# Feed-forward of a two-layer block in split fp32: which of two engines makes the low parts of which weights

## The chip, the cores and the metric

The kernel runs on one core of one Trainium2 chip, in one launch. The metric is device time in microseconds (us). A core has five engines with a queue of instructions each: PE (TensorE) does the matmuls, and PEld is its weight load; DVE (VectorE), ACT (ScalarE) and POOL (GpSimd) work on tiles of 128 partitions; SP (SyncE) issues the DMA transfers. An engine runs its queue in order: an instruction that waits holds up all that stand behind it. Matmuls read SBUF and add into PSUM; DVE and ACT can read PSUM.

## What is computed

Two layers over 512 tokens and 256 context tokens of width 1024, each an attention mixer and a feed-forward, all in fp32. The feed-forward is what the change touches:

```
def swiglu(h, w_in, w_out):
    g, u = jnp.split(h @ w_in, 2, axis=-1)
    return (jax.nn.silu(g) * u) @ w_out
...
        h = h + g2 * swiglu(modulate(h, norm2_g[l], sh2, sc2), ffn_w_in[l], ffn_w_out[l])
        if need_ctx:
            hc = hc + cg2 * swiglu(modulate(hc, norm2_g[l], csh2, csc2), ffn_w_in[l], ffn_w_out[l])
```

The hidden width is 2816, which is 22 tiles of 128. The first layer computes the tokens and the context (768 columns), the second the tokens alone (512).

## The kernel before

**Split products.** Activations lie transposed: features on partitions, tokens along the free axis. To multiply at fp32 precision, each matrix is split into a high part (a cast to fp32r by ScalarE, L901) and a low part (source minus high part, L904), and `mm3` issues three matmuls: high by high (L99), high by low (L100), low by high (L101).

**Seven products for eight.** The input product of a hidden tile f is a 2 by 2 block product, done in Strassen's way with seven products (numbered 1 to 7) of half width instead of eight. `product(n, f)` issues number n. Products 1, 2 and 4 use a quarter of the raw weights as loaded (a11, a12, a22). Products 5, 6, 3 and 7 use a sum: `weights` makes it on VectorE in one tile that is overwritten each time (L926): t = a21 + a22, then t = t - a11, then t = a12 - t, then t = a11 - a21. So a sum can be made only when the split of the sum before it has been read. These tiles are called t, or sq for every third f. The tile of raw weights (1 MB, `ffn_in`, L794) has three buffers, so the load for f + 3 waits for the last reader of f.

**Emptying the accumulators.** VectorE adds the products out of PSUM into the gate and the up part (hs, and q or u): L965 after product 1, L976 after 3, L980 after 7, L982, L985 after 4. The next product into the same accumulator, or into its buffer, waits for them. Two accumulators of this kind (pw) exist, and PE interleaves the products of two tiles. Then hs is split (L115 ScalarE, L116 GpSimd).

**Output weights.** `s2` multiplies pairs of finished hidden tiles by output weights (rawo, L913; on average two splits of 128x512 a hidden tile) into three small accumulators (pb); VectorE empties each into the residual stream (L757: xT for the tokens, ctxT for the context).

**Other work on VectorE.** During the first feed-forward VectorE also computes the second layer's modulation vectors: 64 operations over 128x1024 (L220, junk).

**Who makes the low parts.** `slot` does the split. In the first layer (l = 0) all 192 low parts run on GpSimd: the raw weights of products 1 and 2 need none for f = 0, 1, 2. In the second layer (l = 1), of 198, every fourth call's low part runs on VectorE, whatever is split: 49 of them. In all 341 on GpSimd, 49 on VectorE.

**The order.** The program is written as a list of products and output blocks for each f (the strings in `ffn`), and a list scheduler with its own cost estimates sets the order of each engine's queue. The tiles 0 to 2 have a list of their own; from f = 3 on, two patterns alternate with even and odd f.

Of the kernel before, what the change touches and what calls it, by code (L numbers as in the profile page):

```python
# [6 lines left out]
F32 = mybir.dt.float32  # L7
# [4 lines left out]
ALU = mybir.AluOpType  # L12
# [14 lines left out]
class Builder:  # L27
# [814 lines left out]
    def ffn(self, l):  # L842
        tc, nc, a = self.tc, self.nc, self.a
# [51 lines left out]

        raws, sums, state = {}, {}, {}

        def slot(src, t=None):
            t = ring.tile([P, 2, 512], F32R, name=self.uid("w"), tag="w", bufs=(6, 10)[l]) if t is None else t
            with tc.issue_after(self.first_sq.ins) if self.nslot < 12 else ExitStack():  # L900
                nc.scalar.copy(t[:, 0, :], src)  # L901
            self.nslot += 1
            eng = nc.vector if l == 1 and self.nslot % 4 == 0 else nc.gpsimd
            eng.tensor_tensor(t[:, 1, :], src, t[:, 0, :].bitcast(F32), ALU.subtract)  # L904
            return t

        self.nslot = 0
# [8 lines left out]
        def weights(n, f, plain):  # L916
            if f not in raws:
                raws[f] = self.raws.pop(f) if f < 2 else self.ffn_in(l, f, ring if f % 3 == 2 else self.Rf)
                sums[f] = self.sumsq()[:, :512] if f % 3 == 2 else self.tmp("t")
            r, t = raws[f], sums[f]  # L920
            a11, a12, a21, a22 = [r[:, i * 512:(i + 1) * 512] for i in range(4)]
            for v, x, y, how in ((5, a21, a22, ALU.add), (6, t, a11, ALU.subtract), (3, a12, t, ALU.subtract),
                                 (7, a11, a21, ALU.subtract)):
                if v == n:
                    with tc.issue_after(self.last_diag.ins) if both and f < 3 and n == 5 else ExitStack():
                        nc.vector.tensor_tensor(t, x, y, how)  # L926
            if plain:
                return {1: a11, 2: a12}[n]
            return slot({1: a11, 2: a12, 4: a22}.get(n) if n in (1, 2, 4) else sums[f])

        def more(n, f, ins):

# [4 lines left out]
        def product(n, f):  # L937

            plain = n in (1, 2) and f in self.plain
            w = weights(n, f, plain)  # L940
            st = state.setdefault(f, {})
            if n == 2:
# [58 lines left out]
        def s2_weights(g, m):  # L1001

            if m % 4 == 0:
                outs[g] = load(a["ffn_out"][l, g, :, 256 * m:256 * m + 1024], 1024)
                if g == NF // 2 - 1:
                    f = NF + m // 4
                    pool = ring if f % 3 == 2 else self.Rf
                    self.big = pool.tile([P, 2048], F32R, name=self.uid("raw"), tag="raw", bufs=1 if pool is ring else 2)
            if m % 2 == 0:
                o = m % 4 * 512  # L1010
                t = self.big[:, o:o + 1024].rearrange("p (a b) -> p a b", a=2) if g == NF // 2 - 1 else None
                w2[g] = slot(outs[g][:, m % 4 * 256:m % 4 * 256 + 512], t)
            w = w2[g]
            return [(w[:, 0, c:c + P], w[:, 1, c:c + P]) for c in range(m % 2 * 256, m % 2 * 256 + 256, P)]
# [37 lines left out]
        for off, n in parts:  # L1052
            rest = []
            for m in range(KT):
# [6 lines left out]
                eng = nc.vector if both and m in (2, 3) else nc.gpsimd  # L1061
# [282 lines left out]
```

## Time and profile before

| what | us |
|---|---|
| three runs | 1690.64, 1688.33, 1688.64 (median 1688.64) |
| profiled execution: span from first to last instruction | 1687.1 |
| GpSimd low parts of L904: t 106, raw 105, rawo 74 and 7, sq 49 | 487.8 busy (341 at about 1.43 mean) |
| VectorE waiting in L926 for the weights' DMA | 31.3 (t) |
| ScalarE's casts of t waiting for VectorE's sums | 174.1 |
| first feed-forward, L904 first to last start | 424 to 942 |
| second feed-forward | about 1270 to 1650 |

The profiled execution is a run of its own: the table has its span, and of its whole time the three runs' median, 1.5 us above that span, is the nearest measure. A row of the page's waits reads "engine line <- engine line: total, times, longest": the first stood idle until the second was done. In a timeline row the bracket at the end is the engine's idle time before that instruction and what ended it. In the groups by line, the three numbers of a row are busy time, mean ns of one, and idle time before.

### The profile page before, as it was taken

The numbers are of one execution on the slowest core, as the hardware profiler recorded it, in microseconds if no ns is written. First come the engines' busy times: TensorE is split into PE (matmuls) and PEld (weight loads), VectorE is DVE, ScalarE is ACT, GpSimd is POOL, SyncE is SP. The second block draws the span as 40 slices with busy tenths as digits, with TensorE's granted clock in tenths as the row PEclk, the third lists the DMA queues.
The fourth block names the chain that finished last, engine by engine and source line by source line (L and its number), as shares of the span: only waits on it lengthen the run. The fifth ranks groups of instructions, "written<-read, shape, count | busy, mean of one in ns | idle before, by whom it ended". The sixth has DMA issues, their size and how long they took to land.

```text
span 1687.1 us, 24578 instructions
## 1 busy us (share of the span) xinstructions
PE 1559.4 (92%) x9463; PEld 1363.1 (81%) x9463; DVE 1115.4 (66%) x1994; ACT 725.7 (43%) x1464; POOL 795.6 (47%) x580
## 2 busy tenths in 40 slices
PE   6999989799899899999999998999986998999996
PEld 4776878699689889889999877767776888888886
DVE  4613778855966777667665685765669865666665
ACT  3413676433533333333333345555555444434443
POOL 0562211231575665666655427522116675656663
PEclk9999989999899999999999989999998999999998
DMA  8753100241032333443341112101140332223201
GB/s 314 292 180 136 35 1 1 88 139 62 17 134 79 134 113 113 137 147 127 126 139 49 49 51 76 50 20 38 57 157 7 119 112 77 90 98 108 88 31 50
DMA packets 47957, 161.97 MB, mean 96 GB/s; under 512 B 5472, under 2 KB 9952, under 8 KB 40160
## 3 DMA queue, kind: packets, MB, share of 16 engines
q1 hardware_dynamic: 47696, 160.28, 27.3%
q8 instruction: 74, 1.21, 0.3%
q14 instruction: 43, 0.35, 0.1%
q10 hardware_dynamic: 144, 0.13, 0.0%
HBM read 158.29 MB, written 2.10 MB: 95 GB/s over the span
## 4 chain that ended last, share of the span: by engine, by line
PE 65%; DVE 17%; DMA 5%; POOL 4%; issue 4%; ACT 3%; POOLq 0%; SPq 0%; DVEq 0%; ACTq 0%
PE pb L100 8%; PE pb L99 8%; PE pb L101 8%; PE pw L99 7%; PE pw L100 7%; PE pw L101 7%; DMA raw<-ffn_in 5%; POOL w L904 3%; PE pf L99 2%; PE pb L1199 2%; PE pf L100 2%; PE pf L101 2%; DVE t L926 2%; PE pb L1193 2%; PE pf L349 2%
## 5 line engine op out<-in xcount | busy, mean ns | idle before, releaser
L78 POOL TENSOR_TENSOR w<-raw,w 128x512 fp32r<-128x512 f32 (+1 forms) x84 | 126.6, 1515 | 233.0 <-ACT w L75 210.0
L99 PE MATMUL pw<-ax,w 128*128 128x384 f32 (+2 forms) x640 | 209.6, 332 | 17.8 <-DVE q L980 8.2
L904 POOL TENSOR_TENSOR w<-t,w 128x512 fp32r<-128x512 f32 x106 | 153.2, 1446 | 152.0 <-ACT w L901 150.5
L100 PE MATMUL pw<-ax,w 128*128 128x384 f32 (+2 forms) x640 | 209.0, 327 | 2.1 <-DVE ax L456 1.4
L101 PE MATMUL pw<-ax,w 128*128 128x384 f32 (+2 forms) x640 | 207.0, 326 | 3.1 <-DVE w L904 3.1
L757 DVE SCALAR_TENSOR_TENSOR xT<-pb,mod,xT 128x512 f32<-128x512 f32 (+3 forms) x208 | 144.0, 703 | 68.1 <-PE pb L101 67.7
L99 PE MATMUL pb<-hh,w 128*128 128x512 f32 x480 | 166.3, 361 | 14.3 <-ACT hh L115 7.9
L99 PE MATMUL pw<-T,w 128*128 128x384 f32 (+1 forms) x504 | 159.4, 320 | 18.0 <-DVE hs L976 9.8
L904 POOL TENSOR_TENSOR w<-raw,w 128x512 fp32r<-128x512 f32 x105 | 148.7, 1425 | 56.0 <-ACT w L901 55.8
L100 PE MATMUL pb<-hh,w 128*128 128x512 f32 x480 | 172.8, 362 | 0.7 <-POOL hh L116 0.2
L101 PE MATMUL pb<-hh,w 128*128 128x512 f32 x480 | 168.8, 359 | 0.0
L100 PE MATMUL pw<-T,w 128*128 128x384 f32 (+1 forms) x504 | 160.1, 318 | 5.8 <-POOL T L116 3.7
L901 ACT CAST w<-t 128x512 fp32r<-128x512 f32 x120 | 74.3, 621 | 207.7 <-DVE t L926 174.1
L101 PE MATMUL pw<-T,w 128*128 128x384 f32 (+1 forms) x504 | 159.2, 316 | 0.0
L99 PEld LDWEIGHTS pw<-ax,w 128*128 128x128 f32 x640 | 123.6, 194 | 32.4 <-DVE q L980 12.0
L100 PEld LDWEIGHTS pw<-ax,w 128*128 128x128 f32 x640 | 124.3, 194 | 9.5 <-DVE ax L456 3.1
L101 PEld LDWEIGHTS pw<-ax,w 128*128 128x128 f32 x640 | 124.1, 194 | 6.8 <-DVE w L904 3.3
L904 POOL TENSOR_TENSOR w<-rawo,w 128x512 fp32r<-128x512 f32 x74 | 106.9, 1445 | 40.0 <-ACT w L901 40.0
L99 PEld LDWEIGHTS pw<-T,w 128*128 128x128 f32 x504 | 97.6, 195 | 25.4 <-DVE hs L976 11.8
L99 PEld LDWEIGHTS pb<-hh,w 128*128 128x128 f32 x480 | 89.9, 190 | 27.5 <-ACT hh L115 9.0
L99 PE MATMUL pb<-ax,w 128*128 128x256 f32 (+1 forms) x340 | 104.7, 310 | 3.9 <-ACT w L75 1.6
L100 PEld LDWEIGHTS pw<-T,w 128*128 128x128 f32 x504 | 98.5, 195 | 10.6 <-POOL T L116 5.1
(387 smaller groups left out, 4216.0 us busy)
## 6 DMA issues: line engine op xcount, KB each, us to landing
raw<-ffn_in SPq DMA_DIRECT2D x44, 1024.0 KB, 5.0
ar<-ada SPq DMA_DIRECT2D x24, 1024.0 KB, 7.2
ar<-ada SPq DMA_DIRECT2D x48, 512.0 KB, 3.5
rawo<-ffn_out SPq DMA_DIRECT2D x44, 512.0 KB, 3.8
raw<-odd_out SPq DMA_DIRECT2D x32, 256.0 KB, 2.7
raw<-qk SPq DMA_DIRECT2D x16, 256.0 KB, 7.8
raw<-uv SPq DMA_DIRECT2D x16, 256.0 KB, 2.8
raw<-even_out SPq DMA_DIRECT2D x8, 512.0 KB, 3.5
```

Of the source, the lines that this page charges most:

```text
L78: eng.tensor_tensor(lo, raw, hi.bitcast(F32), ALU.subtract)
L99: mm(out, s[0], m[0], start=start, stop=False, **kw)
L100: mm(out, s[0], m[1], start=False, stop=False, **kw)
L101: mm(out, s[1], m[0], start=False, stop=stop, **kw)
L349: nc.tensor.matmul(ps[32 * q:32 * q + 32, :w], cst[:, k, :], t[:, w * q:w * q + w], start=k == 0, stop=k == KT - 1, skip_group_check=True)
L757: self.nc.vector.scalar_tensor_tensor(h, ps[:, r], self.modcol(l, j, m, who), h, ALU.mult, ALU.add)
L901: nc.scalar.copy(t[:, 0, :], src)
L904: eng.tensor_tensor(t[:, 1, :], src, t[:, 0, :].bitcast(F32), ALU.subtract)
L926: nc.vector.tensor_tensor(t, x, y, how)
L1193: nc.tensor.transpose(pt[:, x * P:(x + 1) * P], es[2 * (x % 2) + x // 2][:, kb * P:(kb + 1) * P], self.ident)
L1199: nc.tensor.matmul(po[64 * h:64 * h + 64, :], V[vb][:, 64 * g:64 * g + 64], t[:, h * TC:h * TC + TC], start=kb == 0, stop=kb == nb - 1, sk ...
```

## The change

`slot` takes the engine as an argument. The split of a sum (products 5, 6, 3, 7) gets VectorE where f > 2, in both layers; everything else (raw weights, output weights, and the sums of f = 0, 1, 2) goes to GpSimd. So 76 low parts of each layer, 152 in all, run on VectorE instead of 49, and 238 on GpSimd instead of 341. The lines behind 903 have a number one lower afterwards.

```
-        def slot(src, t=None):
+        def slot(src, t=None, eng=None):
             t = ring.tile([P, 2, 512], F32R, name=self.uid("w"), tag="w", bufs=(6, 10)[l]) if t is None else t
             with tc.issue_after(self.first_sq.ins) if self.nslot < 12 else ExitStack():
                 nc.scalar.copy(t[:, 0, :], src)
             self.nslot += 1
-            eng = nc.vector if l == 1 and self.nslot % 4 == 0 else nc.gpsimd
-            eng.tensor_tensor(t[:, 1, :], src, t[:, 0, :].bitcast(F32), ALU.subtract)
+            (eng or nc.gpsimd).tensor_tensor(t[:, 1, :], src, t[:, 0, :].bitcast(F32), ALU.subtract)
             return t
...
             if plain:
                 return {1: a11, 2: a12}[n]
-            return slot({1: a11, 2: a12, 4: a22}.get(n) if n in (1, 2, 4) else sums[f])
+            return slot({1: a11, 2: a12, 4: a22}[n]) if n in (1, 2, 4) else slot(t, eng=nc.vector if f > 2 else None)
```

Before, VectorE in the steady part of the first feed-forward, from the L980 of one tile (up part u_6835) over the next tile's first two sums after its start (t_6993 = t - a11, then a12 - t):

```order
L980 TENSOR_TENSOR u_6835<-u_6835,pw_6798 128x384
L220 SCALAR_TENSOR_TENSOR junk_6933,acc_64<-ar_6931,cb_3265 128x1024
L757 SCALAR_TENSOR_TENSOR ctxT_635_3303<-pb_6883,mod_67,ctxT_635_3303 128x256
L982 TENSOR_TENSOR hs_6811<-hs_6811,u_6835 128x384
L757 SCALAR_TENSOR_TENSOR xT_632_3297<-pb_6939,mod_66,xT_632_3297 128x512
L757 SCALAR_TENSOR_TENSOR ctxT_636_3305<-pb_6947,mod_67,ctxT_636_3305 128x256
L926 TENSOR_TENSOR t_6993<-t_6993,raw_6991 128x512
L985 TENSOR_TENSOR hs_6811<-hs_6811,pw_6798 128x384
L926 TENSOR_TENSOR t_6993<-raw_6991,t_6993 128x512
L757 SCALAR_TENSOR_TENSOR xT_632_3297<-pb_6955,mod_66,xT_632_3297 128x512
```

The same place after the change:

```order
L979 TENSOR_TENSOR u_6835<-u_6835,pw_6798 128x384
L220 SCALAR_TENSOR_TENSOR junk_6933,acc_64<-ar_6931,cb_3265 128x1024
L757 SCALAR_TENSOR_TENSOR ctxT_635_3303<-pb_6883,mod_67,ctxT_635_3303 128x256
L903 TENSOR_TENSOR w_7072<-t_6993,w_7072 128x512
L981 TENSOR_TENSOR hs_6811<-hs_6811,u_6835 128x384
L757 SCALAR_TENSOR_TENSOR xT_632_3297<-pb_6939,mod_66,xT_632_3297 128x512
L757 SCALAR_TENSOR_TENSOR ctxT_636_3305<-pb_6947,mod_67,ctxT_636_3305 128x256
L925 TENSOR_TENSOR t_6993<-t_6993,raw_6991 128x512
L984 TENSOR_TENSOR hs_6811<-hs_6811,pw_6798 128x384
L903 TENSOR_TENSOR w_7090<-t_6993,w_7090 128x512
L925 TENSOR_TENSOR t_6993<-raw_6991,t_6993 128x512
L757 SCALAR_TENSOR_TENSOR xT_632_3297<-pb_6955,mod_66,xT_632_3297 128x512
```

Two low parts (w_7072 of product 5, w_7090 of product 6) now stand in VectorE's queue, each ahead of the sum that overwrites what it reads.

Before, VectorE in the steady part of the second feed-forward, at the change from a pair's even tile (hs_14132) to its odd one (hs_14289, u_14309), with the first sum of a later tile (sq_14766, straight from its load):

```order
L976 TENSOR_TENSOR hs_14289<-hs_14289,pw_14276 128x256
L926 TENSOR_TENSOR t_14426<-t_14426,raw_14424 128x512
L985 TENSOR_TENSOR hs_14132<-hs_14132,pw_14119 128x256
L926 TENSOR_TENSOR sq_14766<-raw_14764 128x512
L904 TENSOR_TENSOR w_14503<-t_14426,w_14503 128x512
L980 TENSOR_TENSOR u_14309<-u_14309,pw_14276 128x256
```

After the change:

```order
L981 TENSOR_TENSOR hs_14132<-hs_14132,q_14160 128x256
L925 TENSOR_TENSOR sq_14766<-raw_14764 128x512
L903 TENSOR_TENSOR w_14485<-t_14426,w_14485 128x512
L984 TENSOR_TENSOR hs_14132<-hs_14132,pw_14119 128x256
L925 TENSOR_TENSOR t_14426<-t_14426,raw_14424 128x512
L975 TENSOR_TENSOR hs_14289<-hs_14289,pw_14276 128x256
L903 TENSOR_TENSOR w_14503<-t_14426,w_14503 128x512
L925 TENSOR_TENSOR t_14426<-raw_14424,t_14426 128x512
L903 TENSOR_TENSOR w_14531<-t_14426,w_14531 128x512
L979 TENSOR_TENSOR u_14309<-u_14309,pw_14276 128x256
```

The sum straight from the load (sq_14766) has moved ahead of L984 (the L985 of before), with a low part between them, and two more low parts stand ahead of L979 (the L980 of before).

Before, GpSimd in the opening of the second feed-forward (T tiles are split activations for product 5):

```order
L904 TENSOR_TENSOR w_12004<-t_11869,w_12004 128x512
L904 TENSOR_TENSOR w_12040<-sq_11945,w_12040 128x512
L904 TENSOR_TENSOR w_12082<-t_11869,w_12082 128x512
L904 TENSOR_TENSOR w_12099<-t_11906,w_12099 128x512
L116 TENSOR_TENSOR T_11985<-hm_11488,T_11985 128x256
L116 TENSOR_TENSOR T_11990<-hm_11487,T_11990 128x256
```

After the change:

```order
L903 TENSOR_TENSOR w_12004<-t_11869,w_12004 128x512
L903 TENSOR_TENSOR w_12022<-t_11906,w_12022 128x512
L903 TENSOR_TENSOR w_12040<-sq_11945,w_12040 128x512
L116 TENSOR_TENSOR T_11985<-hm_11488,T_11985 128x256
L116 TENSOR_TENSOR T_11990<-hm_11487,T_11990 128x256
L903 TENSOR_TENSOR w_12082<-t_11869,w_12082 128x512
```

One low part (w_12022) came over from VectorE, and the two T tiles moved ahead of w_12082 and w_12099.

More of the change, by code (lines that the diff above doesn't have):

```diff
@@ L896, in ffn, with slot @@
         raws, sums, state = {}, {}, {}
-        def slot(src, t=None):
+        def slot(src, t=None, eng=None):
             t = ring.tile([P, 2, 512], F32R, name=self.uid("w"), tag="w", bufs=(6, 10)[l]) if t is None else t
@@ L902, in slot @@
             self.nslot += 1
-            eng = nc.vector if l == 1 and self.nslot % 4 == 0 else nc.gpsimd
-            eng.tensor_tensor(t[:, 1, :], src, t[:, 0, :].bitcast(F32), ALU.subtract)
+            (eng or nc.gpsimd).tensor_tensor(t[:, 1, :], src, t[:, 0, :].bitcast(F32), ALU.subtract)
             return t
@@ L928, in weights @@
                 return {1: a11, 2: a12}[n]
-            return slot({1: a11, 2: a12, 4: a22}.get(n) if n in (1, 2, 4) else sums[f])
+            return slot({1: a11, 2: a12, 4: a22}[n]) if n in (1, 2, 4) else slot(t, eng=nc.vector if f > 2 else None)
         def more(n, f, ins):
```

## The prediction

> **What bounds the kernel now.** I read the page's totals first, then the same table cut into the two feed-forwards.
>
> ```profile
> span 1687.1 us, 24578 instructions
> PE 1559.4 (92%) x9463; PEld 1363.1 (81%) x9463; DVE 1115.4 (66%) x1994; ACT 725.7 (43%) x1464; POOL 795.6 (47%) x580
> 560.00:940.00 380.00, 364.89 (x2034) 340.31 (x2033) 259.94 (x384) 127.76 (x232) 234.38 (x155) 0.99 0.34 116
> 1270.00:1380.00 110.00, 92.99 (x592) 83.80 (x592) 94.57 (x133) 53.67 (x116) 74.55 (x55) 0.92 0.22 77
> 1380.00:1640.00 260.00, 244.52 (x1640) 223.83 (x1639) 157.23 (x228) 112.63 (x229) 161.51 (x120) 0.98 0.25 86
> ...
> L976 DVE TENSOR_TENSOR hs<-hs,pw 128x384 f32<-128x384 f32 x16 | 8.9, 554 | 43.4 <-PE pw L101 43.4
> L976 DVE TENSOR_TENSOR hs<-hs,pw 128x256 f32<-128x256 f32 x16 | 6.6, 412 | 2.6 <-PE pw L101 2.6
> ```
>
> The rows with a colon give a stretch, its length, and the busy time of PE, weight load, DVE, ACT and POOL. In the first feed-forward's steady part (560 to 940) PE stands still for 380.00 - 364.89 = 15.1 us; in the second's (1380 to 1640) for 15.5 us; in the second's opening (1270 to 1380) for 17.0 us. L976 runs once a hidden tile, so each steady part holds 16 tiles, or 8 of the pairs in which the products are interleaved. The change adds no matmul and drops none, so it can only win from these gaps, or widen them. The first feed-forward's opening uses the hidden tiles 0 to 2, whose splits stay on GpSimd. PE's waits in the two steady parts:
>
> ```profile
> PE pb L99 <- ACT hh L115: 6.8, 2, 3.5
> PE pb L99 <- DVE xT L757: 4.3, 5, 1.2
> PE pw L99 <- DVE q L980: 2.4, 2, 1.2
> ...
> PE pw L99 <- DVE q L980: 5.1, 4, 2.4
> PE pw L99 <- DVE hs L985: 3.9, 4, 1.2
> PE pw L99 <- DVE hs L976: 3.2, 1, 3.2
> PE pw L99 <- DVE u L980: 2.5, 2, 2.4
> ```
>
> The first three rows are of 560 to 940, the other four of 1380 to 1640 (us in total, times, longest). Nearly all of them name a VectorE instruction that empties an accumulator. So VectorE's lateness, not a late weight, is what costs PE time; not one row names a low part. The question is whether the change makes VectorE earlier or later at those few instructions.
>
> **What a low part costs on each engine.**
>
> ```profile
> L904 POOL TENSOR_TENSOR w<-t,w x106: 1257/1298/2292, 424.1 to 1645.9; 128x512 fp32r<-128x512 f32 x106
> L904 DVE TENSOR_TENSOR w<-raw,w x21: 677/1305/1786, 1275.6 to 1631.6; 128x512 fp32r<-128x512 f32 x21
> L904 DVE TENSOR_TENSOR w<-t,w x14: 673/688/1747, 1280.6 to 1642.8; 128x512 fp32r<-128x512 f32 x14
> DVE t L926: 35.2, 31
> DVE sq L926: 15.4, 12
> ...
> L926 DVE TENSOR_TENSOR t<-t,raw x30: 670/684/2329, 426.0 to 1633.6; 128x512 f32<-128x512 f32 x30
> L926 DVE TENSOR_TENSOR t<-raw,t x30: 673/1758/2323, 435.0 to 1641.2; 128x512 f32<-128x512 f32 x30
> ...
> L901 ACT CAST w<-t x120: 603/621/632, 423.4 to 1645.2; 128x512 fp32r<-128x512 f32 x120
> ```
>
> Durations are least/median/most in ns. Undisturbed, a low part takes 1.30 us on GpSimd and 0.69 on VectorE. The tails show contention: the same sum takes 0.68 or 1.76 us, the same low part 0.69 or 1.75, so an operation with two SBUF inputs that meets a GpSimd operation loses up to some 1.07 us, 1.65 at worst (2.33 - 0.68). The two middle rows are who waited for L904: VectorE stood still for 50.6 us because the next sum overwrites a tile whose low part GpSimd had not finished reading.
>
> **Term 1, first feed-forward, steady part.** All 4 sum splits of a tile leave GpSimd (64 in 16 tiles); VectorE gets 64 x 0.69 = 44 us more against its idle 380.00 - 259.94 = 120 us. The idle that the old order forces on it goes. One instance, VectorE's rows and then PE's:
>
> ```profile
> 687.33 1.50 DVE L926 TENSOR_TENSOR t<-raw 128x512 f32<-128x512 f32 x1 [1.90 <-POOL w L904]
> 688.76 0.54 DVE L980 TENSOR_TENSOR q<-q,pw 128x384 f32<-128x384 f32 x1
> 692.28 0.68 DVE L926 TENSOR_TENSOR sq<-sq,raw 128x512 f32<-128x512 f32 x1
> 692.88 0.54 DVE L985 TENSOR_TENSOR hs<-hs,pw 128x384 f32<-128x384 f32 x1
> 695.08 2.31 DVE L926 TENSOR_TENSOR sq<-raw,sq 128x512 f32<-128x512 f32 x1 [1.65 <-POOL w L904]
> 697.31 0.74 DVE L757 SCALAR_TENSOR_TENSOR xT<-pb,mod,xT 128x512 f32<-128x512 f32 x1
> ...
> 689.35 0.44 PE L99 MATMUL pw<-ax,w 128*128 128x384 f32 x1 [1.22 <-DVE q L980]
> 698.11 0.50 PE L99 MATMUL pb<-hh,w 128*128 128x512 f32 x1 [0.47 <-DVE xT L757]
> ```
>
> The sum waits 1.65 us for GpSimd's low part and then runs 2.31 instead of 0.68, beside GpSimd; L757 stands behind it and PE behind L757. In the new order of the same place (VectorE, first feed-forward, above) a low part stands ahead of the first sum (+0.69), and another, after L984, ahead of the second. First sum 692.97 to 693.65, ScalarE's high part to 694.3 (0.62, beside L984), low part to 695.0, second sum to 695.7, L757 at 695.7 instead of 697.31: 1.6 us early, which closes a gap of 0.47 and those of 1.1 us. Each of the three two-input operations can lose up to 1.07 us to GpSimd, and L757 is later than before when two of them do; GpSimd's busy time falls by 64 x 1.30 = 83 of 234 us, so that this is the rarer case. For the L980 gap (1.22) the 1.90 us wait goes and two lows come ahead of it (1.38), so that closes less surely. The two rows hold 4.3 + 2.4 = 6.7 us. Ends: -6.7 (all closed), and +13 (at each of 8 pairs one 1.65 us stall reaches PE). I take **-5**, near the lower end, since the two instances above both name GpSimd's low part as the idle time that made VectorE late. The 6.8 us behind ScalarE's hh I leave.
>
> **Term 2, second feed-forward, steady part.** Here every fourth split was on VectorE already: 9 splits a tile (7 of the input weights, 2 of the output weights) gave 2.25; now it makes 4. That is 1.75 x 0.69 = 1.2 us a tile more; gone is the wait for GpSimd. But these gaps come from something else:
>
> ```profile
> 1463.51 0.94 DVE L926 TENSOR_TENSOR t<-raw 128x512 f32<-128x512 f32 x1 [1.87 <-DMA raw<-ffn_in]
> 1464.38 1.75 DVE L904 TENSOR_TENSOR w<-sq,w 128x512 fp32r<-128x512 f32 x1
> 1466.05 0.41 DVE L980 TENSOR_TENSOR q<-q,pw 128x256 f32<-128x256 f32 x1
> ...
> 1496.74 0.69 DVE L926 TENSOR_TENSOR t<-raw 128x512 f32<-128x512 f32 x1 [2.88 <-DMA raw<-ffn_in]
> 1497.36 0.41 DVE L985 TENSOR_TENSOR hs<-hs,pw 128x256 f32<-128x256 f32 x1
> ...
> 1466.51 0.39 PE L99 MATMUL pw<-ax,w 128*128 128x256 f32 x1 [2.37 <-DVE q L980]
> 1497.82 0.39 PE L99 MATMUL pw<-ax,w 128*128 128x256 f32 x1 [1.23 <-DVE hs L985]
> ```
>
> A sum that waits for its weights' DMA holds up what stands behind it: in one pair of tiles a low part on VectorE and L980 (PE loses 2.37), in the next L985 alone (1.23). The new order (its lines below 903 are one lower) has one pattern in every pair: L979, L981, the sum behind the DMA, a low part, L984. So L979 is out from behind the DMA, and L984 (the old L985) gets a low part ahead of it. That part's high part is ready, and costs 0.69, or 1.75 contended. On SyncE's queue the load goes out when GpSimd's last low part of the tile three back is done; with the sums gone from GpSimd's queue and ScalarE's casts a step earlier I count it 0.5 us (one cast of 0.62) early. So each pair keeps about 1.25, plus now and then a lock wait: three gaps of 2.37 and the one of 3.2 lose 1.1 each (-4.5), eight pairs gain 0.25 (+2), together **-2.5**. Ends: -7 (the late loads no longer reach PE in the four pairs: half of the 14.7 us of the four rows), and +17 (1.07 lost twice in each of 8 pairs). New on VectorE is its wait for ScalarE: in the new order one low part in four stands right behind its own sum and waits the cast, 0.62 us. Behind it are L964, L975 and L979; two other products' matmuls cover it, unless VectorE comes late already.
>
> **Term 3, opening of the second feed-forward.** Five splits go back to GpSimd: +6.5 us there, -3.4 on VectorE.
>
> ```profile
> 1285.50 3.20 POOL L904 TENSOR_TENSOR w<-t,w 128x512 fp32r<-128x512 f32 x2 [5.61 <-ACT w L901]
> 1289.89 0.58 PE L100 MATMUL pw<-T,w 128*128 128x256 f32 x1 [2.97 <-POOL T L116]
> ```
>
> PE loses 2.97 us since two low parts (3.20) stand ahead of the T tiles; the new order puts the T tiles ahead of them. Against that, one raw low part more goes through GpSimd at 1270 to 1280, where VectorE's tiny operations of the norm wait for it. Ends -3 and +3; I take **-1**. The last group of output weights moves one low part to GpSimd: nothing, since PE works on other products there.
>
> **A rule weighed.** The rows show that contention falls on whole operations (0.69 or 1.75). The Trainium skill, page "SBUF — State Buffer", section "Who interferes with whom", states that a VectorE operation with two SBUF inputs and a GpSimd operation that reads SBUF hold a shared port exclusively, the one that starts second waiting for the first to end. The 1.07 lost agrees, against 1.30 for GpSimd's operation. By that rule the change does not make the two engines work side by side: each moved low part shortens the hold from 1.30 to 0.69, and puts the wait in the queue on which PE depends. Its outcome is the rival on the other side.
>
> **Sum.** -5 - 2.5 - 1 = -8.5: span 1687.1 to 1678.6. The runs took 1688.33 to 1690.64, median 1688.64, which is 1.5 above the profiled span: **1680**.
>
> **The rivals.**
> - *VectorE comes late (slower).* GpSimd loses 16 x 1.75 low parts of 1.30 there, 36 us, and is still busy some 125 of 260 us; a moved low part that meets it takes 1.75, and everything behind it, L984 and L979 above all, goes late. For it: the low part now stands between the late sum and L984. Price: in each of 8 pairs the 1.07 reaches PE twice, +17, less the 5 won in the first feed-forward and 1 in the opening, about +11: 1700; half of it, +5 or so: 1694. It decides once more than about half of these low parts meet GpSimd.
> - *Nothing in sum.* VectorE's waits for GpSimd turn into waits for ScalarE's cast, and what the first feed-forward wins the second loses: -2 to +2, about 1688.
> - *More than I count.* GpSimd's lighter queue also takes most of the lock waits away, the 2.37 gaps and the T wait close entirely: -6.7 - 7 - 3 = -17: 1672.
>
> **How the numbers follow.** Forecast 0.47 (1675 to 1686), VectorE late 0.23, nothing in sum 0.2, more than counted 0.1. The range of 8 in 10 runs from 1672 to 1698: it takes in the larger gain and most of the slower case. About 0.2% (3.4 us) is what a measurement of this kernel can tell from no change. Faster than 1685.3: nearly all of the forecast and the larger gain, 0.55; same: nothing in sum and the forecast's edge, 0.22; slower: 0.23.
>
> **What would show it.** Right: "DVE L926 <- POOL w L904" falls from 50.6 us to what the tiles 0 to 2 have, the gaps of PE behind L757 and L979 in 560 to 940 shrink from 6.7 us to 2 or less, PE waits for L979 in 1380 to 1640 shrink and those for L984 stay at about 1.2 each. Wrong: low parts on VectorE with a median over 1.3 us, waits of "DVE w L903 <- ACT" of tens of us, or new PE waits for pb or pw behind them.

## The result, and the profile after

| kernel | median, us | runs (least to most) | profiled span, us |
|---|---|---|---|
| before, measured with the change | 1689.64 | 4 (1688.33 to 1690.72) | 1687.1 |
| after | 1675.77 | 4 (1672.10 to 1676.44) | 1674.4 |

The ratio after to before is 0.991, interval 0.9892 to 0.9928. The profiled execution of the changed kernel is its run of 1676.23 us. The two profiled executions differ by 12.7 us, where the prediction had 8.5.

The totals at the head of the page of the changed kernel:

```profile
span 1674.4 us, 24582 instructions
PE 1550.9 (93%) x9463; PEld 1358.2 (81%) x9463; DVE 1152.9 (69%) x2097; ACT 729.3 (44%) x1464; POOL 658.4 (39%) x477
```

GpSimd lost 137 us (795.6 before) and VectorE gained 37.5 (1115.4). PE's own busy time fell by 8.5 us (1559.4) at the same 9463 matmuls, which the prediction didn't foresee. The mean granted clock of PE was 0.971 in this execution and 0.969 in that of before, so a part of it is the clock's.

The groups of L903 and L925 in the changed kernel (least/median/most in ns):

```profile
L903 POOL TENSOR_TENSOR w<-raw,w x126: 1261/1296/2246, 464.4 to 1628.7; 128x512 fp32r<-128x512 f32 x126
L903 DVE TENSOR_TENSOR w<-t,w x104: 671/693/1872, 481.3 to 1629.3; 128x512 fp32r<-128x512 f32 x104
...
DVE t L925: 3.0, 2
...
L925 DVE TENSOR_TENSOR t<-raw,t x30: 670/1078/2305, 434.1 to 1622.3; 128x512 f32<-128x512 f32 x30
```

The moved low part takes 0.69 us, as the prediction assumed. The sum a12 - t, made in the tiles called t, has a median of 1.08 us where it had 1.76. The short row is who waited for L903: of VectorE's 50.6 us behind GpSimd 3.0 are left.

PE's waits in the changed kernel, the first row of 560 to 940 us, the others of 1380 to 1640:

```profile
PE pb L99 <- ACT hh L115: 5.3, 2, 3.2
...
PE pw L99 <- DVE hs L984: 5.3, 6, 2.3
PE pw L99 <- DVE q L979: 4.2, 5, 0.9
PE pw L99 <- DVE u L979: 1.9, 2, 1.0
```

Between 560 and 940 us no wait for VectorE is left. In the second feed-forward, the four rows of 14.7 us became three of 11.4.

**Where the time came from.** The span is cut at events that each kernel has. In the feed-forwards it is cut by ScalarE's casts of hh (L115), of which each hidden tile has one (the last has two halves).

| stage | before, us | after, us | difference |
|---|---|---|---|
| to the last emptying of ctxT from pw, ahead of the first feed-forward | 400.7 | 399.8 | -0.9 |
| to the 4th hh of the first feed-forward | 117.1 | 117.5 | +0.4 |
| 4th to 10th hh | 159.2 | 154.2 | -5.0 |
| 10th to last hh | 286.3 | 276.9 | -9.4 |
| to the second mixer's first exponential (L1171) | 80.7 | 84.6 | +3.9 |
| first to last exponential | 190.0 | 190.2 | +0.2 |
| to the 4th hh of the second feed-forward | 120.3 | 123.1 | +2.8 |
| 4th to last but one hh | 304.4 | 299.6 | -4.8 |
| to the end | 28.5 | 28.5 | 0 |

The two rows of the first feed-forward that hold its gain, as windows of before (busy time of PE, weight load, VectorE, ScalarE, GpSimd, then the granted clock):

```profile
517.76:676.95 159.19, 149.13 (x825) 140.04 (x824) 120.09 (x180) 52.05 (x97) 100.00 (x62) 0.98 0.35 119
676.95:963.24 286.29, 278.99 (x1568) 259.15 (x1567) 182.04 (x271) 95.47 (x174) 168.29 (x118) 1.00 0.34 112
```

And of the changed kernel:

```profile
517.26:671.49 154.23, 147.15 (x827) 138.87 (x826) 132.97 (x206) 52.32 (x98) 59.45 (x37) 0.99 0.35 123
671.49:948.35 276.86, 276.73 (x1568) 259.84 (x1567) 191.84 (x315) 95.86 (x175) 110.56 (x73) 1.00 0.34 116
```

The second row of each has the same 1568 matmuls at the same granted clock of 1.00. PE's idle time falls from 286.29 - 278.99 = 7.3 us to 0.1: afterwards PE is busy from end to end, and nothing is left to win there by waits. Its busy time falls too, by 2.3 us; the list of PE's waits doesn't show that. The profile models where a matmul ends, so the split into busy and idle is less sure than the length of the row. In the other row idle time falls by 3.0 us and busy time by 2.0; there the granted clock went from 0.98 to 0.99, an estimate of 159.19 x 0.02 - 154.23 x 0.01 = 1.6 us, which may be most of the 2.0. But e5, e6 and e7 below take 154.4 there at 0.98, as low a clock as before has, so the row's gain isn't the clock's.

The rows of the second feed-forward, before:

```profile
1233.87:1354.15 120.28, 99.74 (x653) 88.72 (x654) 98.32 (x154) 61.32 (x137) 62.30 (x50) 0.91 0.29 103
1354.15:1658.56 304.41, 286.80 (x1913) 261.82 (x1912) 188.78 (x268) 127.41 (x262) 183.72 (x135) 0.98 0.24 82
```

After:

```profile
1223.14:1346.24 123.10, 99.94 (x671) 90.02 (x672) 100.03 (x152) 62.14 (x140) 65.54 (x52) 0.92 0.28 101
1346.24:1645.88 299.64, 283.30 (x1896) 258.47 (x1895) 197.20 (x297) 130.04 (x259) 149.68 (x106) 0.99 0.23 83
```

Here the counts warn the reader: 18 matmuls lie ahead of the border now that lay behind it (671 against 653). At 299.64 / 1896 = 0.158 us they are 2.8 us. At equal work, by this estimate, the opening stayed at 120.3 and the steady part fell to 302.5: 0 and -1.9 us. In the steady part PE's idle time fell from 304.41 - 286.80 = 17.6 us to 16.3, and the granted clock rose from 0.98 to 0.99.

### The profile page after: what moved, and what is told of

Read it like the earlier page. It is cut to its first block, busy times and chain, and to the rows that moved or that the text cites. A ratio compares the mean times of both kernels' runs of the same rounds, so it can differ in the third digit from the quotient of the medians.

```text
span 1674.4 us, 24582 instructions
## 1 busy us (share of the span) xinstructions
PE 1550.9 (93%) x9463; PEld 1358.2 (81%) x9463; DVE 1152.9 (69%) x2097; ACT 729.3 (44%) x1464; POOL 658.4 (39%) x477
## 4 chain that ended last, share of the span: by engine, by line
PE 66%; DVE 16%; DMA 6%; issue 4%; ACT 4%; POOL 4%; POOLq 0%; SPq 0%; DVEq 0%; ACTq 0%
PE pw L99 8%; PE pb L99 8%; PE pw L100 7%; PE pb L100 7%; PE pw L101 7%; PE pb L101 7%; DMA raw<-ffn_in 4%; PE pf L99 3%; PE pf L100 2%; PE pf L101 2%; PE pb L1198 2%; PE pb L1192 2%; POOL w L903 2%; DVE t L925 2%; DVE junk L220 2%
## 5 line engine op out<-in xcount | busy, mean ns | idle before, releaser
L903 POOL TENSOR_TENSOR w<-raw,w 128x512 fp32r<-128x512 f32 x126 | 173.6, 1391 | 152.2 <-ACT w L901 146.0
L903 POOL TENSOR_TENSOR w<-rawo,w 128x512 fp32r<-128x512 f32 x80 | 122.2, 1527 | 198.4 <-ACT w L901 192.2
L757 DVE SCALAR_TENSOR_TENSOR xT<-pb,mod,xT 128x512 f32<-128x512 f32 (+3 forms) x208 | 144.3, 703 | 48.2 <-PE pb L101 47.8
L99 PE MATMUL pw<-T,w 128*128 128x384 f32 (+1 forms) x504 | 159.0, 318 | 17.1 <-DVE hs L975 7.4
L100 PE MATMUL pw<-T,w 128*128 128x384 f32 (+1 forms) x504 | 159.1, 316 | 3.5 <-POOL T L116 1.8
L99 PEld LDWEIGHTS pw<-T,w 128*128 128x128 f32 x504 | 97.3, 194 | 23.6 <-ACT T L115 8.8
L116 POOL TENSOR_TENSOR hh<-hs,hh 128x768 fp32r<-128x768 f32 (+1 forms) x42 | 75.9, 1809 | 85.5 <-ACT hh L115 83.1
L903 DVE TENSOR_TENSOR w<-t,w 128x512 fp32r<-128x512 f32 x104 | 89.1, 857 | 24.4 <-ACT w L901 23.4
```

The source lines that it names most:

```text
L99: mm(out, s[0], m[0], start=start, stop=False, **kw)
L100: mm(out, s[0], m[1], start=False, stop=False, **kw)
L116: return (lo_eng or nc.vector).tensor_tensor(lo, src, hi.bitcast(F32), ALU.subtract)
L757: self.nc.vector.scalar_tensor_tensor(h, ps[:, r], self.modcol(l, j, m, who), h, ALU.mult, ALU.add)
L903: (eng or nc.gpsimd).tensor_tensor(t[:, 1, :], src, t[:, 0, :].bitcast(F32), ALU.subtract)
```

## The experiments

Each expectation was written before its run. The figures of stages are of one profiled execution each; medians and ratios of e1 to e10 come from five rounds beside the kernel before. In the table, "first" is the first feed-forward, the three rows from 400.7 to its last hh together; "to exponential" is the stretch from its last emptying of ctxT to the second mixer's first exponential (17.1 us less than in the table above); "second" is the second feed-forward's opening and steady part together.

| kernel | median, us | ratio to before (interval) | first | to exponential | second |
|---|---|---|---|---|---|
| before | | | 562.6 | 63.6 | 424.7 |
| after | 1675.77 | 0.991 (0.9892 to 0.9928) | 548.6 | 67.5 | 422.7 |
| e1: change in layer 1 alone | 1680.07 | 0.9945 (0.9928 to 0.9962) | 549.3 | 67.1 | 424.1 |
| e2: change in layer 2 alone | 1690.29 | 1.0002 (0.9989 to 1.0014) | 562.3 | 63.7 | 428.1 |
| e3: unsummed weights to VectorE | 1687.70 | 0.9995 (0.9981 to 1.0009) | 556.6 | 67.1 | 422.5 |
| e4: no overwrite, engines as before | 1688.96 | 0.9996 (0.9984 to 1.0008) | 557.6 | 66.6 | 426.5 |
| e5: change, tables loaded first | 1676.89 | 0.9926 (0.9910 to 0.9942) | 548.4 | 64.9 | 422.9 |
| e6: change, opening as before | 1673.95 | 0.9907 (0.9891 to 0.9923) | 548.8 | 67.8 | 417.7 |
| e7: e5 and e6 together | 1672.66 | 0.9904 (0.9887 to 0.9922) | 549.0 | 67.1 | 417.4 |
| e8: e3 and e4 together | 1683.38 | 0.9963 (0.9948 to 0.9978) | 553.8 | 66.8 | 422.8 |
| e9: change, no overwrite | 1687.96 | 0.9977 (0.9961 to 0.9993) | 558.9 | 64.5 | 420.9 |
| e10: e6 and e9 together | 1683.29 | 0.9955 (0.9941 to 0.9969) | 557.9 | 66.3 | 420.4 |

The second feed-forward has the same code in after, e2, e5 and e9, and their profiles spread from 420.9 to 428.1. A difference of a few us between two single profiles in that column says nothing. Before, e1, e3, e4 and e8 split there as before, and they spread from 422.5 to 426.5: the two groups have the same mean to half a us.

### One layer at a time (e1, e2)

e1, against before, beside the new argument of `slot`:

```
-            eng = nc.vector if l == 1 and self.nslot % 4 == 0 else nc.gpsimd
...
+            if eng is None and l == 1 and self.nslot % 4 == 0:
+                eng = nc.vector
...
-            return slot({1: a11, 2: a12, 4: a22}.get(n) if n in (1, 2, 4) else sums[f])
+            return slot({1: a11, 2: a12, 4: a22}[n]) if n in (1, 2, 4) else slot(t, eng=nc.vector if f > 2 and l == 0 else None)
```

e2, against the change:

```
-            return slot({1: a11, 2: a12, 4: a22}[n]) if n in (1, 2, 4) else slot(t, eng=nc.vector if f > 2 else None)
+            return slot({1: a11, 2: a12, 4: a22}[n]) if n in (1, 2, 4) else slot(t, eng=nc.vector if f > 2 and l == 1 else None)
```

> The change in the first feed-forward alone; the second splits as before (every fourth on VectorE). Theory A (the gain is won in the first feed-forward, where VectorE no longer waits for GpSimd's low part before it overwrites the sum) and rival B (it is won there by GpSimd's lighter queue) both expect about the gain that the change had at the start of the second feed-forward, -11 to -12 us, so about 1677 to 1679. Rival C (both layers share the gain evenly) expects -6 to -7, about 1683.

> The change in the second feed-forward alone; the first has all its low parts on GpSimd as before. Theory A and rival B expect -1 to -3 us (1686 to 1688), since from the opening of the second feed-forward to the end the change won only 1 to 2 us. Rival C expects -6 to -7.

e1 is 9.7 us below before (1689.76 beside it), a little less than theories A and B expected, and has the whole gain of the first feed-forward, 549.3 against 548.6. e2 can't be told from before; its -1 to -3 us did not show. So the gain is won in the first layer. What the second layer adds lies between nothing (e2 against before) and some 4 us (the change against e1).

### What in the first feed-forward was removed (e3, e4, e8)

The change does two things there: VectorE no longer waits for GpSimd before it overwrites a sum, and GpSimd has 76 low parts fewer to do. e3 takes 79 other low parts from GpSimd (of raw weights and of some output weights) and leaves the sums', so that the overwrite still waits; against before (the second layer stays as it was):

```
-            return slot({1: a11, 2: a12, 4: a22}.get(n) if n in (1, 2, 4) else sums[f])
+            return slot({1: a11, 2: a12, 4: a22}[n], eng=nc.vector if f > 2 and l == 0 else None) if n in (1, 2, 4) else slot(t)
...
+                w2[g] = slot(outs[g][:, m % 4 * 256:m % 4 * 256 + 512], t, nc.vector if l == 0 and m % 4 == 0 else None)
```

> First feed-forward: the low parts of the unsummed weights (three a tile, f > 2) and of every second output split go to VectorE, those of the sums stay on GpSimd; second feed-forward as before. 79 low parts are moved there instead of the 76 of the change, so GpSimd is relieved as much and VectorE loaded as much, but the sum is still overwritten only after GpSimd has read it. Theory A expects the waits of VectorE's sums for GpSimd to stay (over 30 us) and at most a third of the gain, -4 to +4. Rival B (lighter GpSimd queue, fewer meetings) expects about the time of the first-feed-forward-only kernel, -10 to -12.

e4 leaves the engines of before and takes the overwrite away: sums 6, 3 and 7 are written over quarters of the raw weights that nothing reads any more, and sum 7 is made a step earlier. Against before:

```
-            for v, x, y, how in ((5, a21, a22, ALU.add), (6, t, a11, ALU.subtract), (3, a12, t, ALU.subtract),
-                                 (7, a11, a21, ALU.subtract)):
+            own = l == 0 and f > 2
+            z = {5: t, 6: a11 if own else t, 3: a12 if own else t, 7: a21 if own else t}
+            for v, x, y, how in ((5, a21, a22, ALU.add), (7, a11, a21, ALU.subtract), (6, z[5], a11, ALU.subtract),
+                                 (3, a12, z[6], ALU.subtract)):
-                if v == n:
+                if v == ({6: 7, 7: 0}.get(n, n) if own else n) or own and n == 6 and v == 6:
...
-                        nc.vector.tensor_tensor(t, x, y, how)
+                        nc.vector.tensor_tensor(z[v], x, y, how)
+            t = z.get(n, t)
...
-            return slot({1: a11, 2: a12, 4: a22}.get(n) if n in (1, 2, 4) else sums[f])
+            return slot({1: a11, 2: a12, 4: a22}.get(n) if n in (1, 2, 4) else t)
```

> Engines as before in both layers. In the first feed-forward, for f > 2, the sums of products 6, 3 and 7 are written over raw quarters that are no longer needed (a11, a12, a21) instead of over the sum before, so that no sum has to wait for GpSimd's low part of the sum before; the sum of 7 is made one step earlier. Theory A expects the waits of VectorE's sums for GpSimd to fall below 20 us and -7 to -12 us. Rival B expects no gain, -2 to +2, since GpSimd's queue and the meetings are as before.

By their medians both look like nothing: e4 came out at 1688.96, as rival B expected and theory A did not. By the stages they don't. VectorE's waits for GpSimd between 560 and 940 us, before:

```profile
DVE t L926 <- POOL w L904: 17.4, 15, 2.1
DVE sq L926 <- POOL w L904: 8.0, 6, 1.7
```

In e3:

```profile
DVE t L927 <- POOL w L905: 6.6, 8, 2.1
...
DVE sq L927 <- POOL w L905: 4.4, 4, 1.7
```

In e4:

```profile
DVE sq L928 <- POOL w L904: 0.3, 1, 0.3
```

So 25.4 us before, 11.0 in e3 and 0.3 in e4 (none in the changed kernel). The windows of e4, cut as above:

```profile
521.98:683.71 161.73, 149.33 (x827) 139.95 (x826) 126.08 (x179) 52.44 (x96) 106.29 (x63) 0.98 0.35 118
683.71:959.62 275.91, 275.91 (x1568) 259.87 (x1567) 170.33 (x269) 96.48 (x174) 178.97 (x116) 1.00 0.35 116
```

In the steady row PE is busy from end to end, as in the changed kernel, while GpSimd does all its old work and is busy for 178.97 us, even more than the 168.29 of before. **That separates the two causes: in the steady part the wait before the overwrite alone cost the 9.4 us, and GpSimd's load, once that wait was gone, cost nothing.** e3 agrees from the other side. Its windows, cut at the same events:

```profile
519.45:678.57 159.12, 148.26 (x822) 137.75 (x820) 132.96 (x204) 51.40 (x95) 63.27 (x38) 0.99 0.35 120
678.57:959.24 280.67, 277.07 (x1571) 260.94 (x1572) 213.23 (x318) 96.29 (x177) 106.62 (x71) 1.00 0.34 114
```

In the second of these rows GpSimd is busy for as little as in the changed kernel (106.62 us), and VectorE still waits 4.4 + 3.7 = 8.1 us for it, where the same row of before has 13.4 + 8.0 = 21.4. Some six tenths of the wait are gone, and 5.6 us of the 9.4 are won, six tenths as well: the gain goes with the wait, and not with GpSimd's load.

What spoils e4 lies ahead of that row: 120.0 and 161.7 us where before has 117.1 and 159.2, together +5.4. Something in e4's edit costs time in the first ten tiles: the sums' new place, or sum 7 made earlier. So e4 can't say what won the change 5.0 us in the 4th to 10th tile. e3 has 159.1 there, as before, so it was not GpSimd's lighter load alone; more than that is not shown.

> First feed-forward: the low parts of the unsummed weights and of every second output split on VectorE (79 moved), and the sums written over raw quarters, so that no sum waits for GpSimd; second feed-forward as before. Apart they took 6.0 and 5.0 us off the steady part of the first feed-forward (562.6 us from the last context evacuation out of pw to the last split hidden tile). Theory G (two causes that add: the wait for GpSimd before the overwrite, and GpSimd's load with its meetings) expects about 550 to 552 us there, near the 548.6 of the change. Rival H (one cause, of which each of the two took the same part) expects 555 to 557. The time behind it keeps the 4 us at the mixer's start, so 1680 for G and 1685 for H.

e8 lies between the two expectations, because both added up whole stages. Cut as above it has 120.6, 157.9 and 275.3: the steady part is again at the floor, to which e4's edit alone had brought it, so there was nothing to add there; the first ten tiles have 278.5 against 276.3 before and 281.7 in e4.

### What is left after the change (e9, e10)

These are the change with e4's edit, and e6 with it.

> The change, and in the first feed-forward from the fourth tile on the sums of products 6, 3 and 7 are written over quarters of the raw weights that nothing reads any more, instead of over the tile of the sum before; sum 7 is made a step earlier. Theory G (the change already took away VectorE's wait before the overwrite, since low part and sum now stand in one queue; the sums' place costs nothing more): first feed-forward within 2 us of the change's 548.6 us, in all 1674 to 1678 us. Rival H (what is left of the gain hangs on how early a sum is made, since ScalarE's cast waits for it): first feed-forward 3 to 6 us shorter, 1670 to 1673 us. A third outcome: the raw weights' buffer is held longer by sums written into it, loads come later, first feed-forward 3 us or more longer.

> The kernel of e9 with, in the opening of the second feed-forward (tiles 0 to 2), every fourth low part back on VectorE as before the change. Theory G: first feed-forward within 2 us of 548.6, opening 117 to 119 us (e6 and e7 had 118.0 and 117.4; the change 123.1), in all 1672 to 1675 us, no better than e6 and e7 by more than 2 us. Rival H: 1667 to 1671 us.

Of e9's expectation only the third outcome came, and its reason is not shown. e10 missed both of its outcomes for the same loss: 1683.29 us and 557.9 in the first feed-forward. The windows of e9:

```profile
520.17:683.39 163.22, 150.83 (x825) 140.43 (x824) 132.96 (x205) 52.75 (x97) 62.37 (x37) 0.97 0.34 117
683.39:960.38 276.99, 276.08 (x1568) 259.82 (x1567) 187.72 (x313) 96.43 (x174) 105.94 (x72) 1.00 0.35 116
```

The steady row is that of the change to 0.1 us: with VectorE's wait gone, writing the sums elsewhere brings nothing there. The 4th to 10th tile take 163.2 instead of 154.2, with 5.3 us more idle time and a granted clock of 0.97 instead of 0.99 (an estimate of 163.22 x 0.03 - 154.23 x 0.01 = 3.4 us). Most of the added idle time is behind VectorE's L757, where it empties a small accumulator into xT: PE waits 5.7 us for it there, 1.2 in the change. SyncE's wait for the readers of the raw weights doesn't explain it: between 440 and 950 us it went from 45.4 us (behind GpSimd) to 50.4 (43.1 behind GpSimd and 7.3 behind VectorE). What makes VectorE late in those tiles when the sums lie in the raw weights stays open. The profiled execution of e9 took 1683.15, less than its median, so the typical loss is larger than the windows show.

### The second feed-forward's opening (e6)

Against the change:

```
+            if eng is None and l == 1 and self.early and self.nslot % 4 == 0:
+                eng = nc.vector
...
+            self.early = f < 3
```

> The change, but in the second feed-forward every fourth split of the tiles 0 to 2 has its low part on VectorE again, as before. Theory F (the opening of the second feed-forward lost about 3 us because the five splits given back to GpSimd make VectorE's small norm operations and the first products wait) expects the stretch from the last exponential to the fourth split hidden tile to fall from 123.1 to about 120.3 us, and the time by about 3 us, to 1673. Rival (noise of one profile, or the new order of the norm chain) expects 123 us and no gain.

The opening fell from 123.1 to 118.0 us, with the border back at 653 matmuls (at equal work from 120.3), and the second feed-forward in all from 422.7 to 417.7. The three kernels with this edit, e6, e7 and e10, have 417.4 to 420.4 there, less than each of the nine others (420.9 to 428.1); from e9 to e10 it is only 0.5. The trace shows one wait that the edit takes away. VectorE's timeline in the changed kernel, at the norm ahead of the second feed-forward:

```profile
1258.91 0.16 DVE L156 TENSOR_SCALAR sm<-pb 128x2 f32<-128x2 f32 x1
...
1260.53 1.25 DVE L128 TENSOR_SCALAR sm<-sm 128x2 int32<-128x2 int32 x1
1261.82 1.22 DVE L130 TENSOR_TENSOR sm<-sm 128x2 f32<-128x2 f32 x1
1263.07 1.19 DVE L131 SCALAR_TENSOR_TENSOR sm<-sm,sm 128x2 f32<-128x2 f32 x1
...
1269.17 1.19 DVE L130 TENSOR_TENSOR sm<-sm 128x2 f32<-128x2 f32 x1
1270.39 0.16 DVE L131 SCALAR_TENSOR_TENSOR sm<-sm,sm 128x2 f32<-128x2 f32 x1
...
1270.78 0.48 DVE L165 TENSOR_SCALAR q<-ident,sm 128x128 f32<-128x128 f32 x2
```

GpSimd in the same time:

```profile
1258.70 7.98 POOL L903 TENSOR_TENSOR w<-raw,w 128x512 fp32r<-128x512 f32 x6 [20.66 <-ACT w L901]
1266.64 2.48 POOL L903 TENSOR_TENSOR w<-t,w 128x512 fp32r<-128x512 f32 x2
1269.08 1.26 POOL L903 TENSOR_TENSOR w<-sq,w 128x512 fp32r<-128x512 f32 x1
```

PE's waits between 1262 and 1274 us:

```profile
PE pb L175 <- DVE q L165: 8.1, 1, 8.1
```

An operation on 128x2 takes 0.16 us alone and 1.2 beside GpSimd, about as long as one of GpSimd's low parts there (2.48 us for two). Eight of these stand in a chain, and GpSimd has nine low parts in a row to set against them. PE waits 8.1 us for the chain's end. At the same place of the kernel before, GpSimd has seven:

```profile
1270.14 7.25 POOL L904 TENSOR_TENSOR w<-raw,w 128x512 fp32r<-128x512 f32 x5 [20.34 <-ACT w L901]
1277.36 1.28 POOL L904 TENSOR_TENSOR w<-t,w 128x512 fp32r<-128x512 f32 x1
1278.60 1.29 POOL L904 TENSOR_TENSOR w<-sq,w 128x512 fp32r<-128x512 f32 x1
```

There six of the norm's operations take 1.2 us, PE has products to do meanwhile (58 matmuls between the norm's first and second matmul lines, L149 and L175, against 36 after), and it waits for nothing but a low part, 3.1 us. The chain itself became only 1.0 us longer: from L149's start to L165's it takes 12.8 us before (1268.42 to 1281.20) and 13.8 after (1256.98 to 1270.78). The rest of PE's wait comes from the 22 matmuls that no longer stand between the two lines. The wait of 8 us for L165 is in all four kernels with the whole change in this layer (after, e2, e5, e9) and not in e6, e7 and e10, where those matmuls are back and the chain takes 12.8 us. So a few low parts are better left on VectorE here; why the scheduler then orders PE otherwise was not followed up, and what e6 won behind the opening (some 2.7 us of its 5.0) isn't explained by this wait.

### The second mixer's start (e5, e7)

Nothing of the change touches it, and it became 3.9 us longer. In before and e2 the loads of two tables (cos and sin) are issued ahead of the last weights of V; after the change they come behind them. e5 puts them ahead again; e7 does the same, with e6's edit. Against the change:

```
+                self.last_tab = nc.sync.dma_start(tabs[-1], a[n])
...
+            with tc.issue_after(self.last_tab.ins) if kq else ExitStack():
+                W = self.blocks(a["v1"][kq], step=256)
```

> The change, with the loads of cos and sin issued ahead of the second half of the V weights in the second layer (as the order had them, roughly, before the change). Theory D (the change lost 4 us at the start of the second mixer since the scheduler put these loads behind a V load that waits for a free buffer, so that the rope and all behind it come late) expects the stretch from the last ctxT evacuation to the first exponential of the second mixer to fall from 67.5 to about 63.6 us, and the time to about 1672. Rival E (those 4 us are a clock dip or something else that comes with denser work before it) expects 67 us there and about 1676.

> Both of the two kernels above together. If D and F hold and add: about 63.6 and 120.3 us in the two stretches, and 1676 - 4 - 3 = about 1669, faster than the change. If only one holds: about 1672 to 1673.

e5 fell to 64.9 us, but e7, with the tables ahead too, stayed at 67.1, and e9, with the tables behind as in the change (the load of cos is issued at 1005.33 us), took 64.5. So the order of the loads isn't the cause. Two things differ, the granted clock (the third number from the end) and the matmuls in the stretch, before and in the changed kernel:

```profile
980.30:1043.90 63.60, 56.28 (x322) 48.28 (x321) 43.52 (x87) 29.80 (x49) 31.25 (x24) 0.92 0.23 72
965.40:1032.90 67.50, 59.20 (x327) 50.26 (x326) 44.62 (x87) 29.71 (x49) 32.49 (x24) 0.90 0.21 71
```

By these rows a clock below 1.00 is worth (1 - 0.92) x 63.60 = 5.1 us before and (1 - 0.90) x 67.50 = 6.8 after, an estimate of 1.7 of the 3.9 us. PE's idle time grew by 1.0 us (7.3 to 8.3), and five matmuls more lie in the stretch. e5 and e7 differ there in little but the clock: both have 326 matmuls there and the same waits of PE; at a clock of 0.95 it took 64.9 us, at 0.90 67.1.

One dip can be seen by itself, some 50 us after the first feed-forward's last emptying. The ten us from there in e7:

```profile
1017.60:1027.60 10.00, 7.39 (x26) 5.65 (x25) 5.63 (x8) 4.53 (x8) 5.69 (x4) 0.83 0.28 79
```

And in e9, at the same distance:

```profile
1027.40:1037.40 10.00, 7.39 (x33) 5.81 (x32) 5.61 (x8) 4.50 (x8) 5.72 (x4) 1.00 0.24 79
```

All engines are equally busy, but PE gets 26 matmuls done at 0.83 and 33 at 1.00. The same kind of matmul takes 0.63 us in e7's row, where the clock dips, and 0.39 in e9's:

```profile
1024.46 0.63 PE L99 MATMUL pf<-ax,w 128*128 128x512 f32 x1
1034.71 0.39 PE L99 MATMUL pf<-ax,w 128*128 128x512 f32 x1
```

The clock is 1.00 there in before, e2 and e9 (63.6, 63.7, 64.5 us) and 0.83 in all the others (64.9 to 67.8). This dip can take (1 - 0.83) x 10 = 1.7 us, so it is not all of the 3.9. No run set the clock, and why it dips in some of the kernels is open: the same wait of PE, 2.6 us for qf (L244), stands ahead of it in e7 and in e9.

## Why the prediction was right, and where it wasn't

**Direction and range.** It forecast faster, 1680.0 in 1672 to 1698; the kernel took 1675.77. Three terms were expected to give -8.5 us; the profiles differ by -12.7: -14.0 in the first feed-forward, -1.9 in the second, +3.9 at the second mixer's start, and -0.7 in the rest. That the sum came within some 4 us is partly luck: the first term brought 9.0 us more than it was given, the other two show no gain beyond the spread, and 3.9 us were lost at a place that is not in the sum.

**Term 1 (-5) had the mechanism and too small a size: -14.0.** Its step, that VectorE's wait for GpSimd makes the emptying of accumulators late, is what e4 shows for the steady part (-9.4): without that wait it is at PE's floor whatever the engines. For the 4th to 10th tile (-5.0) the mechanism is not shown. The mis-sized step is "The two rows hold 4.3 + 2.4 = 6.7 us", taken as the most that there was to win. Between the 4th hh and the last, PE's idle time fell by 3.0 + 7.2 = 10.2 us, and its busy time by 2.0 + 2.3 = 4.3 at nearly the same number of matmuls, some 1.6 of it with the clock. That second part appears in no list of waits. It shows when a window's length is divided by its matmuls: 286.29 / 1568 = 0.1826 us before, 0.1766 in the changed kernel. The 5.0 us of the 4th to 10th tile came on top: both rows lie wholly behind them, and PE's waits there, for hh (6.8 us, 5.3 after) and ctxT (2.0, 0.6 after), were not in the term. The prediction's upper bound of its gain, -6.7, was not a bound, and the rival "more than I count" had it too.

**Term 2 (-2.5): the number is near, but no run shows the gain.** At equal work the steady part of the second feed-forward fell by 1.9 us. Its steps can be read in the waits: L984's and L979's rows are 11.4 us for 14.7, no wait behind L975 is left, and those for L979 are at most 1.0 us each where they were 2.4; one for L984 is 2.3, where about 1.2 was foreseen. But PE's idle time in the steady part is 16.3 us for 17.6, while e2, with the same code, has 19.7 and e1, with that of before, 16.5; and the clock's 0.99 for 0.98 is worth up to 304.41 x 0.02 - 299.64 x 0.01 = 3.1 us by estimate, more than the 1.9. The whole run of e2 lies at nothing. That the size came near is luck as far as these runs go.

**Term 3 (-1): its two parts were right, and a third was missing.** The T wait closed from 3.0 to 0.7 us, as foreseen. The other step, "VectorE's tiny operations of the norm wait for it", made the chain 1.0 us longer, about the one low part that was counted. What was not counted is that PE has 36 matmuls instead of 58 to do meanwhile: it waits 8.1 us for the chain, where it waited 3.1 for a low part, and e6, which takes that wait away, is 5.0 us shorter in the second feed-forward. At equal work the opening came out at 0.

**Not in the sum:** the +3.9 us at the second mixer's start. The prediction looked for changes only where the change moves instructions.

**The rivals.** "VectorE comes late" fell: of the low parts that VectorE now makes, 8 of 63 between 560 and 940 us took over 1.2 us, and 7 of 60 between 1380 and 1640; the rival needed more than half. Its new waits for ScalarE's casts came, 9.7 us in the one stretch and 16.5 in the other, at most 1.9 us at a time. The prediction named tens of us as a sign of being wrong; that sign was badly chosen, for in both stretches no wait of PE names a low part. "Nothing in sum" is outside the interval for the whole, though it is what the second feed-forward shows. "More than I count" (1672) is as near to the measured 1675.77 as the forecast is; its own steps, GpSimd's lighter queue above all, are not what e3 and e4 show for the steady part. The rule of the Trainium skill, page "SBUF — State Buffer", section "Who interferes with whom", that of a VectorE operation with two SBUF inputs and a GpSimd operation that reads SBUF the one which starts second waits the other out, agrees with the 1.2 us of the norm's 0.16 us operations; it didn't decide this case, since VectorE's low parts seldom took longer in the steady part (8 of 63).

## What to carry to other kernels

When one engine overwrites what another still reads, putting both on one queue can be worth more than the work it shifts: here 0.69 us a low part on VectorE bought off a wait that cost 9.4 us of a steady part of 286. Size such a gain by the window's length per matmul, compared with a stretch where PE is never idle, and not by PE's listed waits alone. Compare the granted clock of two windows before reading a few us as a gain. And look for a chain of tiny operations beside another engine's run of large ones: here eight of 0.16 us took 1.2 each.

## What was not expected of the hardware

- With equal matmuls at a granted clock of 1.00, a stretch with 7.3 us of idle time was 9.4 us longer than one with 0.1. PE's busy time was 278.99 us in the one and 276.73 in the other, with the ends of matmuls modelled, so where the other 2 us lie isn't sure.
- Eight 128x2 operations of 0.16 us took about 1.2 us each beside GpSimd, 10.3 us from 1260.53 to L165's start at 1270.78.
- The granted clock, averaged over ten us at the same place, was 0.83 in some kernels and 1.00 in others, with all engines equally busy (7.39 us of PE in 10 both times).

The fastest version was e7, 1672.66 us (0.9904, interval 0.9887 to 0.9922). Its interval overlaps that of the change, so that it is better is not certain.
